# Multiply and GELU over 16 MB: x resident in SBUF, y in a ring, one transfer queue, stores behind all loads

## Chip, core and metric

One core of one Trainium2 chip. The metric is the device time of one execution in microseconds. A ratio is the mean time of one kernel's fast runs over the mean time of the other's fast runs of the same rounds, so it is not quite the ratio of the medians that are quoted.

## The reference

```python
def setup_inputs():
    batch, dim = 1024, 4096
    ...                                   # x and y: float32 [1024, 4096], 16.8 MB each

def reference(x, y):
    z = x * y
    return (0.5 * z * (1 + np.tanh(np.sqrt(2 / np.pi) * (z + 0.044715 * z ** 3)))).astype(np.float32)
```

It is elementwise. 33.55 MB have to come in and 16.78 MB have to go out.

## The kernel before

Each of the 128 partitions holds eight rows of the input, 32768 numbers (128 KiB). The kernel walks over them in seven tiles of 4096 columns and four of 1024. Loads are issued by the sync engine, stores by the scalar engine, and the framework places the semaphores.

```python
def _process_tile(nc, sbuf, tile_f, x_r, y_r, out_r, c0, c1):
    ts_ = c1 - c0
    x_tile = sbuf.tile([128, tile_f], x_r.dtype)
    y_tile = sbuf.tile([128, tile_f], y_r.dtype)
    nc.sync.dma_start(out=x_tile[:, :ts_], in_=x_r[:, c0:c1])
    nc.sync.dma_start(out=y_tile[:, :ts_], in_=y_r[:, c0:c1])
    nc.vector.tensor_mul(out=x_tile[:, :ts_], in0=x_tile[:, :ts_], in1=y_tile[:, :ts_])
    nc.scalar.activation(out=x_tile[:, :ts_], in_=x_tile[:, :ts_],
                         func=mybir.ActivationFunctionType.Gelu_apprx_tanh)
    nc.scalar.dma_start(out=out_r[:, c0:c1], in_=x_tile[:, :ts_])

    # ... in the kernel:
    big_sbuf = ctx.enter_context(tc.tile_pool(name="big", bufs=3))      # 4096 columns: 16 KB rows
    small_sbuf = ctx.enter_context(tc.tile_pool(name="small", bufs=8))  # 1024 columns: 4 KB rows
    # seven big tiles, then four small ones
```

## Time and profile before

| | before |
|---|---|
| time, median of 3 | 123.86 us (123.77 to 123.91) |
| span of the profiled execution | 122.5 us |
| DMA queues | 2 (loads, stores) |
| data packets | 2688 of 16 KB, 1536 of 4 KB |
| vector / scalar engine busy | 29% / 25% |

The span is divided into 40 slices; a digit is the busy share in tenths. GB/s counts a packet's bytes in the slice in which the packet starts. The lines themselves stand in the prediction.

### The profile page before, as it was taken

How to read it: one execution, taken by the hardware profiler on the slowest of the kernel's cores; microseconds unless marked ns; L12 is line 12 of the kernel's file. 1: busy time of each engine (PE TensorE's matmuls, PEld its weight loads, DVE VectorE, ACT ScalarE, POOL GpSimd, SP SyncE). 2: the span in 40 equal slices, each digit the busy share in tenths (PEclk: the TensorE clock that was granted, in tenths of full speed). 3: DMA queues.
4: the chain of work that ended last, by engine and by line, in shares of the span. 5: the costliest groups of instructions: out<-in, count | busy, mean ns of one | idle time of the engine just before them, and what ended most of it. 6: DMA issues, size and time to landing. Idle time of an engine off the chain costs nothing.

```text
span 122.5 us, 134 instructions
## 1 busy us (share of the span) xinstructions
DVE 35.8 (29%) x11; ACT 30.7 (25%) x12; POOL 0.2 (0%) x4
## 2 busy tenths in 40 slices
DVE  0000770590000580068000085019300039555000
ACT  4000029009100019001900004700650000884200
POOL 0000000000000000000000000000000000000000
DMA  4999999989999999999999999999999999999994
GB/s 112 428 433 428 439 439 433 369 337 439 439 433 428 433 428 428 428 433 428 428 433 439 439 433 433 428 428 433 433 428 428 428 417 407 411 413 455 397 423 164
DMA packets 4752, 50.33 MB, mean 411 GB/s; under 512 B 528, under 2 KB 528, under 8 KB 2064
## 3 DMA queue, kind: packets, MB, share of 16 engines
q1 hardware_dynamic: 3168, 33.56, 65.7%
q10 hardware_dynamic: 1584, 16.78, 32.2%
HBM read 33.55 MB, written 16.78 MB: 411 GB/s over the span
## 4 chain that ended last, share of the span: by engine, by line
DMA 76%; DVE 8%; ACT 7%; SPq 1%; issue 1%; DVEq 0%
DMA y_tile<-in_y_dram 30%; DMA out_dram<-x_tile 24%; DMA x_tile<-in_x_dram 22%; DVE x_tile L18 8%; ACT x_tile L20 7%; SPq L15 1%; SPq L16 0%; DVEq L18 0%
## 5 line engine op out<-in xcount | busy, mean ns | idle before, releaser
L18 DVE TENSOR_TENSOR x_tile<-x_tile,y_tile 128x4096 f32<-128x4096 f32 (+1 forms) x11 | 35.8, 3261 | 77.4 <-DMA y_tile<-in_y_dram 77.4
L20 ACT ACTIVATE x_tile<-x_tile 128x4096 f32<-128x4096 f32 (+1 forms) x11 | 29.4, 2684 | 82.8 <-DVE x_tile L18 82.4
L20 ACT ACT_TABLE_LOAD x1 | 1.3, 1283 | 0.7 <-PEq L87 0.7
L87 POOL MEMSET const-bfloat16-1.0<- 128x1 bf16 x1 | 0.1, 101 | 0.0
L87 POOL MEMSET const-uint8-127<- 128x1 uint8 x1 | 0.1, 101 | 0.0
L87 POOL MEMSET const-float32-0.0<- 128x1 f32 x1 | 0.1, 98 | 0.2 <-issue 0.2
L87 POOL MEMSET const-float32-1.0<- 128x1 f32 x1 | 0.1, 98 | 0.0
## 6 DMA issues: line engine op xcount, KB each, us to landing
x_tile<-in_x_dram SPq DMA_DIRECT2D x7, 2048.0 KB, 16.3
y_tile<-in_y_dram SPq DMA_DIRECT2D x7, 2048.0 KB, 20.7
out_dram<-x_tile ACTq DMA_DIRECT2D x7, 2048.0 KB, 13.8
x_tile<-in_x_dram SPq DMA_DIRECT2D x4, 512.0 KB, 21.2
y_tile<-in_y_dram SPq DMA_DIRECT2D x4, 512.0 KB, 20.5
out_dram<-x_tile ACTq DMA_DIRECT2D x4, 512.0 KB, 8.6
```

The costliest lines, as they stand in the source:

```text
L15: nc.sync.dma_start(out=x_tile[:, :ts_], in_=x_r[:, c0:c1])
L18: nc.vector.tensor_mul(out=x_tile[:, :ts_], in0=x_tile[:, :ts_], in1=y_tile[:, :ts_])
L20: nc.scalar.activation(out=x_tile[:, :ts_], in_=x_tile[:, :ts_], func=mybir.ActivationFunctionType.Gelu_apprx_tanh,)
L87: nc = _bacc.Bacc("TRN2", target_bir_lowering=False, num_devices=1)
```

## The change

The intent: rows as long as possible, fewer packets, no second queue, no store between loads. All of x stays in SBUF and is overwritten in place by the result. Only y needs a ring (of 16384 columns), whose two halves are loaded again after the multiplies that read them. Waits are written by hand inside one critical section.

```diff
-    nc.sync.dma_start(out=x_tile[:, :ts_], in_=x_r[:, c0:c1])
-    nc.sync.dma_start(out=y_tile[:, :ts_], in_=y_r[:, c0:c1])
-    nc.vector.tensor_mul(...)
-    nc.scalar.activation(...)
-    nc.scalar.dma_start(out=out_r[:, c0:c1], in_=x_tile[:, :ts_])
+X_LOADS = [(0, 16384), (16384, 32768)]
+Y_LOADS = [(0, 16384, 0), (16384, 24576, 0), (24576, 32768, 8192)]   # columns, place in the ring
+STEP = 4096
+STORES = [(0, 16384), (16384, 32768)]
 ...
+    with tc.tile_critical(no_gpsimd_drain=True):
+        xs = nc.alloc_sbuf_tensor("xs", [P, total_f], F32).ap()
+        ys = nc.alloc_sbuf_tensor("ys", [P, Y_RING], F32).ap()
 ...
+        load_x(0)
+        load_y(0)
+        load_x(1)
+        for i in (1, 2):
+            nc.sync.wait_ge(sem_mul, (Y_LOADS[i][1] - Y_LOADS[1][0]) // STEP)
+            load_y(i)
 ...
+            for c in range(a, b, STEP):
+                nc.vector.tensor_mul(...).then_inc(sem_mul, 1)
+                nc.scalar.wait_ge(sem_mul, n)
+                nc.scalar.activation(...).then_inc(sem_act, 1)
+        for i, (a, b) in enumerate(STORES):
+            nc.sync.wait_ge(sem_act, b // STEP)
+            nc.sync.dma_start(out=out_r[:, a:b], in_=xs[:, a:b]).then_inc(sem_o[i], 16)
```

More of the change, by code (lines that the diff above doesn't have):

```diff
@@ L7 @@
 from concourse._compat import with_exitstack
-def _process_tile(nc, sbuf, tile_f, x_r, y_r, out_r, c0, c1):
-    ts_ = c1 - c0
-    x_tile = sbuf.tile([128, tile_f], x_r.dtype)
-    y_tile = sbuf.tile([128, tile_f], y_r.dtype)
-    nc.sync.dma_start(out=x_tile[:, :ts_], in_=x_r[:, c0:c1])
-    nc.sync.dma_start(out=y_tile[:, :ts_], in_=y_r[:, c0:c1])
-    nc.vector.tensor_mul(out=x_tile[:, :ts_], in0=x_tile[:, :ts_], in1=y_tile[:, :ts_])
-    nc.scalar.activation(
-        out=x_tile[:, :ts_],
-        in_=x_tile[:, :ts_],
-        func=mybir.ActivationFunctionType.Gelu_apprx_tanh,
-    )
-    nc.scalar.dma_start(out=out_r[:, c0:c1], in_=x_tile[:, :ts_])
+F32 = mybir.dt.float32
+GELU = mybir.ActivationFunctionType.Gelu_apprx_tanh
+X_LOADS = [(0, 16384), (16384, 32768)]
+Y_LOADS = [(0, 16384, 0), (16384, 24576, 0), (24576, 32768, 8192)]
+STEP = 4096
+STORES = [(0, 16384), (16384, 32768)]
+Y_RING = 16384
 @with_exitstack
@@ L44 @@
     total_f = x_r.shape[1]
-    big_tiles = [4096] * 7
-    small_tiles = [1024] * 4
-    if sum(big_tiles) + sum(small_tiles) != total_f:
-        big_tiles = []
-        remaining = total_f
-        while remaining >= 4096 * 2:
-            big_tiles.append(4096)
-            remaining -= 4096
-        small_tiles = []
-        while remaining > 0:
-            ts_ = min(1024, remaining)
-            small_tiles.append(ts_)
-            remaining -= ts_
-    big_f = max(big_tiles) if big_tiles else 1024
@@ L61, with load_x, load_y @@
-    small_f = max(small_tiles) if small_tiles else 1024
-    big_sbuf = ctx.enter_context(tc.tile_pool(name="big", bufs=3))
-    small_sbuf = ctx.enter_context(tc.tile_pool(name="small", bufs=8))
-    c0 = 0
-    for ts_ in big_tiles:
-        _process_tile(nc, big_sbuf, big_f, x_r, y_r, out_r, c0, c0 + ts_)
-        c0 += ts_
-    for ts_ in small_tiles:
-        _process_tile(nc, small_sbuf, small_f, x_r, y_r, out_r, c0, c0 + ts_)
-        c0 += ts_
+    with tc.tile_critical(no_gpsimd_drain=True):
+        xs = nc.alloc_sbuf_tensor("xs", [P, total_f], F32).ap()
+        ys = nc.alloc_sbuf_tensor("ys", [P, Y_RING], F32).ap()
+        sem_x = [nc.alloc_semaphore(f"sem_x{i}") for i in range(len(X_LOADS))]
+        sem_y = [nc.alloc_semaphore(f"sem_y{i}") for i in range(len(Y_LOADS))]
+        sem_o = [nc.alloc_semaphore(f"sem_o{i}") for i in range(len(STORES))]
+        sem_mul = nc.alloc_semaphore("sem_mul")
+        sem_act = nc.alloc_semaphore("sem_act")
+        def load_x(i):
+            a, b = X_LOADS[i]
+            nc.sync.dma_start(out=xs[:, a:b], in_=x_r[:, a:b]).then_inc(sem_x[i], 16)
+        def load_y(i):
+            a, b, r = Y_LOADS[i]
+            nc.sync.dma_start(
+                out=ys[:, r : r + b - a], in_=y_r[:, a:b]
+            ).then_inc(sem_y[i], 16)
+        load_x(0)
[4 more added lines that the diff above has]
+            load_y(i)
+        n = 0
+        for i, (a, b, r) in enumerate(Y_LOADS):
+            for j, (xa, xb) in enumerate(X_LOADS):
+                if xa <= a < xb:
+                    nc.vector.wait_ge(sem_x[j], 16)
+            nc.vector.wait_ge(sem_y[i], 16)
+            for c in range(a, b, STEP):
+                nc.vector.tensor_mul(
+                    out=xs[:, c : c + STEP],
+                    in0=xs[:, c : c + STEP],
+                    in1=ys[:, r + c - a : r + c - a + STEP],
+                ).then_inc(sem_mul, 1)
+                n += 1
+                nc.scalar.wait_ge(sem_mul, n)
+                nc.scalar.activation(
+                    out=xs[:, c : c + STEP], in_=xs[:, c : c + STEP], func=GELU
+                ).then_inc(sem_act, 1)
+        for i, (a, b) in enumerate(STORES):
+            nc.sync.wait_ge(sem_act, b // STEP)
+            nc.sync.dma_start(out=out_r[:, a:b], in_=xs[:, a:b]).then_inc(sem_o[i], 16)
+        for i in range(len(STORES)):
+            nc.sync.wait_ge(sem_o[i], 16)
```

## The prediction

> **What bounds the kernel now.** I read the page first, for who is busy, then the rates in chosen stretches, then the chain and the waits to see who waits for whom. The slices and the traffic, from the page:
>
> ```profile
> DVE  0000770590000580068000085019300039555000
> ACT  4000029009100019001900004700650000884200
> ...
> DMA  4999999989999999999999999999999999999994
> GB/s 112 428 433 428 439 439 433 369 337 439 439 433 428 433 428 428 428 433 428 428 433 439 439 433 433 428 428 433 433 428 428 428 417 407 411 413 455 397 423 164
> DMA packets 4752, 50.33 MB, mean 411 GB/s; under 512 B 528, under 2 KB 528, under 8 KB 2064
> ...
> HBM read 33.55 MB, written 16.78 MB: 411 GB/s over the span
> ```
>
> The two compute engines work in islands (29% and 25% of the span); the 16 DMA engines are full from the second slice to the last but one. The bytes are exactly x, y and the output once each, so none can be saved. What is left to gain is the distance between the mean of 411 GB/s and the plateau of about 430. The dips are in the first slice, in slices 8 and 9, from slice 33 on, and in the last. Rates in stretches (columns: stretch, its length, busy time of vector, scalar and pool engine with instructions, clock, DMA share, GB/s):
>
> ```profile
> 0.00:5.00 5.00, 0.00 (x0) 1.28 (x1) 0.20 (x4) 1.00 0.70 239
> 5.00:21.00 16.00, 4.42 (x1) 3.45 (x1) 0.00 (x0) 1.00 1.01 432
> 21.00:28.00 7.00, 4.42 (x1) 0.83 (x2) 0.00 (x0) 1.00 0.99 370
> 28.00:97.00 69.00, 17.70 (x4) 17.42 (x5) 0.00 (x0) 1.00 1.01 431
> 98.00:111.00 13.00, 8.01 (x4) 5.92 (x4) 0.00 (x0) 1.00 1.02 419
> 111.00:115.00 4.00, 1.22 (x1) 1.81 (x2) 0.00 (x0) 1.00 1.00 428
> 116.50:120.25 3.75, 0.00 (x0) 0.00 (x0) 0.00 (x0) 1.00 1.02 419
> ```
>
> 5 to 21 holds loads alone, 28 to 97 loads and stores mixed, 111 to 115 stores of 16 KB rows alone: 432, 431, 428. Loads, stores and a mixture share one limit; they don't add up to more, and mixing costs nothing visible. In 98 to 111 (loads of 4 KB rows) and from 116 (stores of 4 KB rows) it is 419. The dip at 21 to 28 is where the first store is issued:
>
> ```profile
> 21.20 0.38 ACTq L26 DMA_DIRECT2D out_dram<-x_tile  x1
> ```
>
> The chain of waits is made of transfers, and what the vector engine waits for is a landing y:
>
> ```profile
> DMA 76%; DVE 8%; ACT 7%; SPq 1%; issue 1%; DVEq 0%
> ...
> L18 DVE TENSOR_TENSOR x_tile<-x_tile,y_tile 128x4096 f32<-128x4096 f32 (+1 forms) x11 | 35.8, 3261 | 77.4 <-DMA y_tile<-in_y_dram 77.4
> ```
>
> The 8% and 7% of compute in that chain are no cost: while they run, other transfers keep the DMA full. The load queue's own waits, 78.7 us for stores that must free a buffer, look alarming, but the DMA share of 1.01 in the same stretches says that enough was always queued. So the bound is DMA throughput, and the time is bytes over line rate plus a few losses.
>
> **What the Trainium skill says.** "DMA: Bandwidth & Descriptors", section "Where 436 GB/s comes from", derives 16 ports x 32 B x 850 MHz = 435.2 GB/s; this trace's 431 to 432 fits just beneath it. The same section lets HBM bind HBM-to-SBUF traffic at about 358; the trace's 432 contradicts that for this lone core, and the measurement decides. The same page, section "Issuing engines are not separate DMA queues", says that transfers issued from different engines interleave on the same 16 DMA engines; the trace agrees (432 with one queue active, 431 with two). So going to one queue neither gains nor loses rate. "SBUF — State Buffer", section "SBUF size: 192, 224, or 256?", leaves about 208 KiB usable per partition: all of x (128 KiB) and the 64 KiB ring are 192 KiB and fit, which is why y alone needs a ring; no trace shows this. "ScalarE: Activation LUTs", section "What ACT_TABLE_LOAD costs", gives 186 ns + 0.833 ns per element with immediates, 3.60 us for 4096; the trace's 3.616 us agrees, and these instructions don't change.
>
> **The change, part by part.** First the ledger of the present span against the line rate of 435.2. Bytes: 50.33 MB / 435.2 = 115.65 us. Start: 0 to 5 us shows 239 GB/s = 1.195 MB, but a packet counts where it starts, so about half of 16 packets of 16 KB (0.13 MB) belongs later; 1.06 MB are 2.45 us of work, so 2.55 us are lost (0.73 until the first issue, the rest is the way to the first packet and its long first service). Plateau: 16 us at 432 lose 0.12, 69 us at 431 lose 0.67. The dip: 7 us x (1 - 370/435.2) = 1.05. Small tiles: 13 us at 419 lose 0.48; the rest of the end to 120 about 0.3. Sum 5.2, so at 120.8 the DMA engines are done on average; from there to the end of 122.5 are 1.7 us. In the trace the last packet ends at 121.27, its landing is reported at 121.75, and barriers fill the last 0.79.
>
> Larger rows. A 16 KB packet takes 16 x 16384 / 432 = 606.8 ns on its engine, of which 602.4 are the line rate: 4.5 ns fixed (estimate). A 4 KB packet at 419 takes 156.4, of which 150.6 are the line rate: 5.8 ns. So about 5 ns per packet, whatever its size. Before there are 2688 + 1536 data packets, 264 per engine: 1.3 us. After, if a row stays one packet: five transfers of 128 rows of 64 KB and two of 32 KB, 896 rows, 56 per engine: 0.3 us. Gain 1.0 us. It lies on the bounding path throughout, because the engines are always busy.
>
> The first store moved behind all loads, into the same queue. The dip of 1.05 us (about 1.0 beyond the plateau's own loss) follows the first DMA that the scalar engine's queue ever issued. The later stores that begin after a pause show no dip: those issued at 49.23 and 61.28 fall into slices 18 and 22 with 433 and 439. I choose to read it as a first use of that queue, which the change does away with: gain 1.0 us. It is the least certain term, since it could be the first write to HBM instead.
>
> One queue, in order. Is it ever empty? Data flows from about 2.6 us at 434 GB/s: y0 is in by 2.6 + 16.8/0.434 = 41 us, x1 by 60.5, y1 by 70, y2 by 80, the first store by 99. y1 needs two multiplies after y0 (41 + 2 x 4.43 = 50, slack 10 us), y2 four (59, slack 11), the first store the fourth GELU (59 + 3.6 = 63, slack 17), the last store the eighth: 80 + 2 x 4.43 + 3.62 = 93, about 1 us more for landing notices, slack 5 us before 99. No bubble. Eleven multiplies and GELUs become eight equal ones, all hidden.
>
> Start and end. First issue, first packet and its latency stay: 2.55. The end: a smaller spread of the 16 engines with one queue (-0.15), perhaps one more barrier at the end of the hand-placed section (+0.2): 1.75 instead of 1.7.
>
> Sum after: 2.55 + 115.65 + 0.3 (packets) + 0.05 (completion writes) + 1.75 = 120.3 us of span. The unprofiled time before is 123.86 - 122.54 = 1.32 above the span; kept, this gives **121.6 us**, 1.8% faster.
>
> **The rivals.**
> 1. The dip comes back where loads turn to stores, near 80 us. For it: the dip of before coincides with the first write of any kind, and slices 8 and 9 show slow loads before a store's data moves. Against: later returns to storing cost nothing. Time 122.6.
> 2. Rows of 64 KB are cut into packets of 16 KB or less. Against: rows of 16 KB are one packet today (2688 packets for 21 transfers of 128 rows). Cut to 16 KB: 192 per engine x 5 ns = 0.96, so +0.65, 122.3; cut to 32 KB: +0.2.
> 3. Compute is exposed, because loads and stores no longer overlap and the first multiply waits until 41 us instead of 13.09. Against: every slack above is over 4 us, and mixing bought no bandwidth. Were the last store late after all, each us of lateness would be a us of time, 124 or more.
> 4. The two queues' mixture itself was a loss, or the hand-placed semaphores shorten the path noticeably. Against: 431 mixed, 432 alone, and the waits between instructions are hundredths of a us. At most 0.3 us, 121.3.
>
> **Range and chances.** Two per cent below 123.86 is 121.4. The floor of this argument (no barrier added, no spread of the engines, no dip) is 2.5 + 115.65 + 0.35 + 1.27 + 1.32 = 121.1. I give the first-use reading 65%, centred on 121.6 with 0.3 either way; rivals 1 and 2 25%, 122.2 to 122.7; a bubble 5%; something better than my floor 5%. That leaves some 28% under 121.4. Predicted 121.6 us, range 121.0 to 122.6; faster by over 2% 0.28, within 2% 0.70, slower 0.02.
>
> **What would show it.** 896 data packets and 7 x 16 completion writes, about 1010 in all, would confirm the rows; four times as many, rival 2. A rate of about 434 in stretches inside the loads and inside the stores confirms the 5 ns per packet; 431 refutes it. 80 us or so is the place of rival 1: a stretch of 7 us at 370 there is the dip. DMA share at 1.0 from 5 to 118 us confirms that there is no bubble; a chain in which the last store waits for a GELU refutes it. The first rate window, 0 to 5 us, should again lack 2.5 us of work, and the last 1.7 us should look as before. If the start is later because a 64 KB row takes longer to get going, or the gap between span and time is not 1.3 us, the sum is wrong by that much.

## The result

123.41 us (123.32 to 123.48, 4 runs) against 123.83 (123.77 to 123.91, 4 runs): ratio 0.9965, interval 0.9951 to 0.9979. That is the same at 2%, and faster by a third of one per cent. The direction and the class were as predicted; the size was not. 121.6 was forecast with a range of 121.0 to 122.6, so the miss is 1.8 us. All outputs are right.

The page of the kernel after, the lines that answer to those shown of before:

```profile
span 121.6 us, 80 instructions
...
DMA  9777977797789779978999999997997799779970
GB/s 345 345 345 345 690 345 345 345 690 345 345 388 647 345 345 453 582 345 345 431 431 431 431 453 410 345 517 345 431 604 345 345 474 560 345 345 560 474 345 0
DMA packets 1008, 50.33 MB, mean 414 GB/s; under 512 B 112, under 2 KB 112, under 8 KB 112
...
DMA 52%; DVE 22%; ACT 3%; issue 0%; SPq 0%; DVEq 0%
```

1008 packets are 896 rows and 7 x 16 completion writes: a row of 64 KB is one packet, as assumed. The 345s and 690s, and the 7s of the DMA line, are no stutter. A packet of 64 KB takes 2.4 us, a slice 3.04 us, and packets are counted where they start, so a slice sees one or two packets per engine. With such rows the stretch has to be long, or the landings (the moments at which a transfer is reported complete) have to be read instead. The vector engine's instructions give them away, because each group begins when a y lands. From the timeline of the kernel after (start, length, instruction, count, idle time before it and what ended it):

```profile
42.10 17.43 DVE L70 TENSOR_TENSOR xs<-xs,ys 128x4096 f32<-128x4096 f32 x4 [42.10 <-DMA ys<-in_y_dram]
71.16 8.76 DVE L70 TENSOR_TENSOR xs<-xs,ys 128x4096 f32<-128x4096 f32 x2 [11.63 <-DMA ys<-in_y_dram]
81.86 8.76 DVE L70 TENSOR_TENSOR xs<-xs,ys 128x4096 f32<-128x4096 f32 x2 [1.94 <-DMA ys<-in_y_dram]
```

The second part of y (4.19 MB, in the same queue behind x) landed at 71.16, the third (4.19 MB) at 81.86: 10.70 us, where 4.19 MB at 434 GB/s take 9.66. So a full microsecond was lost between the two, shortly before the first store moves. The stretches of the same trace show where (columns as in the prediction):

```profile
40.00:76.00 36.00, 22.27 (x6) 14.85 (x5) 0.00 (x0) 1.00 0.98 422
76.00:83.00 7.00, 5.06 (x2) 6.28 (x2) 0.00 (x0) 1.00 0.99 375
83.00:119.00 36.00, 7.62 (x2) 7.80 (x3) 0.00 (x0) 1.00 1.01 437
```

7 us at 375, with the engines' share at 0.99: they are not idle, their packets are slow. The packet records in the kept trace, which no view prints one by one, show which: 16 load packets of 32 KB, as many as there are engines, start between 77.57 and 77.95 us and take 2.06 us in the mean in place of 1.21. The load packets after them are back at 1.21 to 1.28, and the first store packet, at 80.76, takes the usual 2.42. So the time is lost on loads, about 3 us before a store's data moves. In the kernel before it is much the same: the slow packets, starting from 23.09 to 26.48 us, are all of the load queue, and the first store packet starts at 24.99. This is the dip of before (7 us at 370), moved from 21 to 77 us. It is rival 1 of the prediction. And the first issue is later than the 0.73 us of before:

```profile
0.94 0.38 SPq L48 DMA_DIRECT2D xs<-in_x_dram  x1
```

A third discrepancy is in the times. The prediction added 1.32 us to the span, from a time of 123.86 and a profile of 122.54. But the time of each later run is recorded together with its own span, and time less span is 1.72 to 1.83 in all of them, whatever the kernel; the spans of the kernel before are 121.8 to 122.3 there. So the profile that was studied must have been of an execution about 0.5 us longer than the ones that the 123.86 came from. That half microsecond was counted as something the change would remove.

### The profile page after: what moved, and what is told of

Its sections match the earlier page's. It is cut to its first block, busy times and chain, and to the rows that moved or that the text cites. A ratio compares the mean times of both kernels' runs of the same rounds, so it can differ in the third digit from the quotient of the medians.

```text
span 121.6 us, 80 instructions
## 1 busy us (share of the span) xinstructions
DVE 35.0 (29%) x8; ACT 30.2 (25%) x9; POOL 0.2 (0%) x4
## 2 busy tenths in 40 slices
DMA packets 1008, 50.33 MB, mean 414 GB/s; under 512 B 112, under 2 KB 112, under 8 KB 112
## 3 DMA queue, kind: packets, MB, share of 16 engines
q1 hardware_dynamic: 1008, 50.33, 96.9%
## 4 chain that ended last, share of the span: by engine, by line
DMA 52%; DVE 22%; ACT 3%; issue 0%; SPq 0%; DVEq 0%
DMA ys<-in_y_dram 52%; DVE xs L70 22%; ACT xs L77 3%; SPq L48 0%; DVEq L68 0%; SPq L111 0%; SPq L37 0%
## 5 line engine op out<-in xcount | busy, mean ns | idle before, releaser
L70 DVE TENSOR_TENSOR xs<-xs,ys 128x4096 f32<-128x4096 f32 x8 | 35.0, 4422 | 55.7 <-DMA ys<-in_y_dram 55.7
L77 ACT ACTIVATE xs<-xs 128x4096 f32<-128x4096 f32 x8 | 28.9, 3617 | 63.2 <-DVE xs L70 63.2
```

The lines of the kernel that those rows point to most:

```text
L70: nc.vector.tensor_mul(out=xs[:, c : c + STEP], in0=xs[:, c : c + STEP], in1=ys[:, r + c - a : r + c - a + STEP],).then_inc(sem_mul, 1)
L77: nc.scalar.activation(out=xs[:, c : c + STEP], in_=xs[:, c : c + STEP], func=GELU).then_inc(sem_act, 1)
```

## The experiments

Three theories of the dip were on the table: A, the first write to HBM; B, the turn from loads to stores in one queue; C, the first use of the scalar engine's queue (the prediction's choice). The "turn" is the change from loads to stores. To read the runs, each of them by one profiled execution: in the changed kernel and its variants, the idle time of the vector engine before its last group of multiplies is about 1.9 us with a full dip before the last y landed and about 0.9 without one.

### e1: an early small store in the changed kernel

```diff
+        nc.vector.memset(warm[:, :], 0.0).then_inc(sem_w, 1)            # warm: [128, 128]
+        nc.scalar.wait_ge(sem_w, 1)
+        nc.scalar.dma_start(out=out_r[:, 0:128], in_=warm[:, :]).then_inc(sem_wd, 16)
         load_x(0)
 ...
+        nc.sync.wait_ge(sem_wd, 16)      # before the real stores
```

> The changed kernel with one 64 KB store of zeros into the first output columns, issued on the scalar engine's queue at the very start and waited for before the real stores. Theory A (the dip near 78 us comes from the first write of the kernel to HBM, whatever queue): the dip near 78 us vanishes, its 0.9 us is paid under the start or not at all, time about 122.5 to 122.7 (0.8 us less than 123.4). Theory B (the dip comes from the turn from loads to stores in one queue, or from the first store on the sync queue): the dip stays at 77 to 80 us and the time stays at 123.4 to 123.6.

Measured: 123.55 us (ratio to before 0.9982). The last group of multiplies, in its timeline:

```profile
81.96 8.76 DVE L77 TENSOR_TENSOR xs<-xs,ys 128x4096 f32<-128x4096 f32 x2 [1.86 <-DMA ys<-in_y_dram]
```

The dip stayed. A small first write doesn't pay it off.

### e2, e3, e6: fresh queue or first write, in the kernel before

The making of the tile `warm` is left out of the cuts.

```diff
 e2
+    nc.scalar.dma_start(out=warm[:, :], in_=x_r[:, 0:128])                        # a 64 KB load
 e3, behind the first x and y load
+        nc.sync.dma_start(out=out_r[:, total_f - 128 : total_f], in_=warm[:, :])  # a 64 KB store
 e6, at the start
+    nc.scalar.dma_start(out=out_r[:, total_f - 128 : total_f], in_=warm[:, :])
```

> The kernel before with one 64 KB load issued on the scalar engine's queue at the start, so that this queue is no longer fresh when the first store comes at 21 us. Theory A (first write): the dip at 23 to 26 us stays, time 123.9 to 124.1. Theory C (first use of that queue, the prediction's reading): the dip vanishes, time about 122.9 to 123.1.

> The kernel before with one 64 KB store of zeros on the sync queue behind the first x and y load, so that it runs at about 12 us among loads; the scalar queue stays fresh until 21 us. Theory A (first write): the dip moves to about 9 to 13 us and none is left at 23 to 26; time within 0.2 of 124.0. Theory C (first use of the scalar queue): no dip near 12, the dip stays at 23 to 26.

> The kernel before with one 64 KB store of zeros on the scalar queue at the start. Theory F: the dip at 23 to 26 us vanishes, time 123.1 to 123.4. Theory G: it stays, time 123.9 to 124.1.

Measured: 124.00, 123.97 and 123.93 us, with before at 123.83, 123.83 and 123.79. The stretch of the dip in e2:

```profile
21.00:28.00 7.00, 4.43 (x1) 0.85 (x2) 0.00 (x0) 1.00 1.01 386
```

in e3:

```profile
21.00:28.00 7.00, 4.43 (x1) 0.69 (x2) 0.00 (x0) 1.00 1.01 391
```

and in e6:

```profile
21.00:28.00 7.00, 4.42 (x1) 0.82 (x2) 0.00 (x0) 1.00 1.02 393
```

All three have the dip where it was, 0.6 to 0.7 us deep (7 x (1 - 390/431)), a little less than the 1.0 of the first profile. The queue had carried a load (e2) or a store (e6) already, so C falls. HBM had been written already (e3, e6), so A in its simple form falls as well.

### e5, e7: the same queue, and half a megabyte

Both are the changed kernel without the hand-placed section (e4, below). In e5 a 64 KB store went over the one queue that carries everything. It was meant to be the first transfer, but the framework put it behind the first x load, at about 21 us. In e7 512 KB went over the scalar queue from the start; packets of 4 KB took turns with load packets of 64 KB, so they were spread over 7 to 23 us (packet records).

```diff
 e5
+    nc.sync.dma_start(out=out_r[:, 0:128], in_=warm[:, :])
 e7
+    nc.scalar.dma_start(out=out_r[:, 0:1024], in_=warm[:, :])
```

> The changed kernel without the hand-placed section (122.85 us, run e4), with one 64 KB store of zeros as the first transfer of the sync queue, the queue that carries everything. Theory F (the first store of each queue costs about 0.9 us, and the early stores so far went over the other queue): the dip near 78 us vanishes, time 122.0 to 122.4. Theory G (the first large store costs it, however small ones went before): the dip stays, time 122.9 to 123.2.

> Run e4 with a 512 KB store of zeros (4 KB rows) on the scalar queue at the start; it adds 1.2 us of traffic. Theory G with a threshold that half a megabyte passes: a dip in the first 10 us, none near 78, time about 124.0 or, if the dip hides under the start, 123.3. Theory F or a higher threshold: the dip stays near 78, time about 124.1.

Measured: 122.88 and 123.96 us. The last group in e5:

```profile
81.66 8.76 DVE L53 TENSOR_TENSOR xs<-xs,ys 128x4096 f32<-128x4096 f32 x2 [1.59 <-DMA ys<-in_y_dram]
```

and in e7:

```profile
82.66 8.76 DVE L53 TENSOR_TENSOR xs<-xs,ys 128x4096 f32<-128x4096 f32 x2 [1.58 <-DMA ys<-in_y_dram]
```

The dip stays in both, at 0.7 us. Theory F (each queue's first store) falls. e7 leaves open whether its stores were too few, too slow or in the wrong queue.

### e10, e11: is it once, or at every turn?

```diff
 e10, behind the second x load (at 60 us), then y, then the rest
+    nc.sync.dma_start(out=out_r[:, 0:8192], in_=xs[:, 0:8192])
 e11, behind the first x load (at 21 us)
+    nc.sync.dma_start(out=out_r[:, 0:3072], in_=warm[:, :])        # 1.5 MB of zeros
```

> Run e4 with the first 4 MB of the output stored between the second x load and the third y load (at 60 us), then 19 us of loads, then the rest. Theory N (once per execution): a dip at 57 to 61 us, none at the second turn near 89. Theory P (each start of storing after a long stretch of loads alone): dips at both, time 0.9 us over 122.9, 123.8.

> Run e4 with 1.5 MB of zeros (12 KB rows) stored behind the first x load, at 21 us, in the same queue; 3.6 us more traffic. Theory N: a dip at about 18 to 22 us and none at the turn 55 us later, near 82; time 126.5. Theory P: dips at both, time 127.3.

Measured: 123.11 and 126.89 us. For comparison the same groups in e4, which has no early burst:

```profile
41.89 17.43 DVE L53 TENSOR_TENSOR xs<-xs,ys 128x4096 f32<-128x4096 f32 x4 [41.89 <-DMA ys<-in_y_dram]
...
71.03 8.76 DVE L53 TENSOR_TENSOR xs<-xs,ys 128x4096 f32<-128x4096 f32 x2 [11.71 <-DMA ys<-in_y_dram]
...
81.76 8.76 DVE L53 TENSOR_TENSOR xs<-xs,ys 128x4096 f32<-128x4096 f32 x2 [1.97 <-DMA ys<-in_y_dram]
```

e10:

```profile
81.76 8.76 DVE L53 TENSOR_TENSOR xs<-xs,ys 128x4096 f32<-128x4096 f32 x2 [22.30 <-DMA ys<-in_y_dram]
...
91.45 8.76 DVE L53 TENSOR_TENSOR xs<-xs,ys 128x4096 f32<-128x4096 f32 x2 [0.93 <-DMA ys<-in_y_dram]
```

e11:

```profile
46.85 17.43 DVE L53 TENSOR_TENSOR xs<-xs,ys 128x4096 f32<-128x4096 f32 x4 [42.80 <-DMA ys<-in_y_dram]
...
75.92 8.76 DVE L53 TENSOR_TENSOR xs<-xs,ys 128x4096 f32<-128x4096 f32 x2 [11.63 <-DMA ys<-in_y_dram]
...
85.55 8.76 DVE L53 TENSOR_TENSOR xs<-xs,ys 128x4096 f32<-128x4096 f32 x2 [0.88 <-DMA ys<-in_y_dram]
```

In e10 the second y landed at 81.76. Without the early store it was 71.03 (e4), and 4.19 MB more take 9.66: 80.69. So the early store met the dip (1.07 us late), and the turn 19 us of loads later did not: from 81.76 to 91.45 are 9.69 us. In e11 the first y landed 4.96 us after the 41.89 of e4, for 3.62 us more traffic; the real turn 55 us later shows no dip (85.55 - 75.92 = 9.63). In these runs the cost is paid once per execution, and an earlier burst buys it off. Theory B, in the form of "at every turn", falls.

### e9: small tiles first

```diff
-    for ts_ in big_tiles: ...
-    for ts_ in small_tiles: ...
+    for ts_ in small_tiles: ...
+    for ts_ in big_tiles: ...
```

> The kernel before with its four 1024-column tiles first, so that the first stores are 512 KB and come at about 8 us, mixed with loads. Theory N (the dip belongs to the first start of storing at speed, of any size from half a megabyte): one dip at about 6 to 12 us, none later. Theory S (it comes where a long backlog of loads meets the first large store): dip at the first 2 MB store, near 20 to 30 us. Time between 123.3 and 124.3.

Measured: 130.69 us, far out of what was expected, for a reason that has nothing to do with the dip:

```profile
9.00:15.00 6.00, 2.53 (x3) 2.11 (x2) 0.00 (x0) 1.00 1.06 417
...
35.00:41.00 6.00, 2.92 (x1) 0.00 (x0) 0.00 (x0) 1.00 0.99 401
...
115.00:124.00 9.00, 3.73 (x1) 3.62 (x1) 0.00 (x0) 1.00 0.13 56
```

With a large tile last, its multiply and its GELU (4.4 + 3.6 us) run with nothing left to transfer: 9 us at 56 GB/s. The small tiles at the end of the kernel before earn about 7 us. As for the dip, a weaker one came at the first 512 KB stores and a second at the first 2 MB store, 401 GB/s. So one clean dip was wrong here; with a gentle beginning it comes in two parts.

### e14, e15: rate or volume, write or read

```diff
 e14, in place of the 1.5 MB of e11: 512 KB to HBM
+    nc.sync.dma_start(out=out_r[:, 0:1024], in_=warm[:, :])
 e15: the 1.5 MB of e11, but to SBUF (the second x load overwrites it later)
+    nc.sync.dma_start(out=xs[:, 16384 : 16384 + 3072], in_=warm[:, :])
```

> Run e11 with 512 KB of zeros in place of 1.5 MB (4 KB rows), at full rate at 21 us. If rate sets the dip off, the dip is at 19 to 22 us and none near 79. If volume does (above half a megabyte), none at 21 and one near 79. Time 124.1 to 124.3 either way.

> Run e11 with the 1.5 MB copied from SBUF to SBUF in place of stored to HBM. If bulk reading of SBUF by the DMA engines sets the dip off, it is at 19 to 22 us and none at the turn near 82. If writing to HBM does, none at 21 and one at 82. Time about 126.5 to 127.

Measured: 124.05 and 126.80 us. e14:

```profile
44.39 17.43 DVE L53 TENSOR_TENSOR xs<-xs,ys 128x4096 f32<-128x4096 f32 x4 [42.47 <-DMA ys<-in_y_dram]
...
83.11 8.76 DVE L53 TENSOR_TENSOR xs<-xs,ys 128x4096 f32<-128x4096 f32 x2 [0.89 <-DMA ys<-in_y_dram]
```

e15:

```profile
46.96 17.43 DVE L53 TENSOR_TENSOR xs<-xs,ys 128x4096 f32<-128x4096 f32 x4 [42.91 <-DMA ys<-in_y_dram]
...
85.67 8.76 DVE L53 TENSOR_TENSOR xs<-xs,ys 128x4096 f32<-128x4096 f32 x2 [0.85 <-DMA ys<-in_y_dram]
```

e14: the first y is 2.50 us later than in e4 for 1.21 us of traffic, and the real turn is clean. So half a megabyte is enough if it comes as a burst in the loads' queue; e7 had the same bytes, but spread out, taking turns with loads, and in the scalar queue. No run parts these two differences. The queue alone doesn't decide, since the stores of the kernel before and of e13 (below) go over the scalar queue and meet the dip. e15 is the surprise: before a copy that never writes to HBM, the first y is 5.07 us later for 3.62 of traffic (a packet of the copy takes 0.46 us, as one of e11's stores does), and the turn at 82 us is without a dip. So writing to HBM isn't needed. What e11, e14 and e15 share is a burst of transfers whose source is SBUF, behind a stream of loads. A change of tensor alone isn't enough: in e4 the loads pass from x to y near 22 us at an unchanged 434 GB/s (packet records).

### e17, e18: can it be paid in the slow first microseconds?

```diff
 in the changed kernel, as the very first transfer; e17: 512 columns (256 KB), e18: 1024 (512 KB)
+        nc.sync.wait_ge(sem_w, 1)
+        nc.sync.dma_start(out=xs[:, 16384 : 16384 + W], in_=warm[:, :]).then_inc(sem_wd, 16)
         load_x(0)
         load_y(0)
+        nc.sync.wait_ge(sem_wd, 16)
         load_x(1)
```

> The changed kernel (123.41 us) with a 256 KB copy from SBUF to SBUF as the very first transfer. It costs 0.6 us of traffic and about 0.5 us of later start. If it pays off the dip and the pay-off hides in the slow start of the first loads: no dip near 79, time 123.0 to 123.4. If it pays but does not hide: 124.0 to 124.6. If 256 KB do not set it off: dip near 79, 124.3 to 124.6.

> The same with 512 KB: 1.2 us of traffic and about 1 us of later start. Hidden: 124.0 to 124.5 and no dip near 79; not hidden: 125.0 to 125.5.

Measured: 124.99 and 126.03 us, worse than every expectation. The last group of e18:

```profile
84.50 8.76 DVE L77 TENSOR_TENSOR xs<-xs,ys 128x4096 f32<-128x4096 f32 x2 [2.17 <-DMA ys<-in_y_dram]
```

The dip is there in full, and e17's last group, with 1.69 us of idle time before it, has most of it. 512 KB in a burst ahead of the first load bought nothing off, while 512 KB behind a load did (e14). So the burst has to come behind a running stream of loads, as far as these two runs show; e14 stored to HBM and e18 copied to SBUF.

### e4: the changed kernel without the hand-placed section

```diff
-    with tc.tile_critical(no_gpsimd_drain=True):
-        xs = nc.alloc_sbuf_tensor("xs", [P, total_f], F32).ap()
-        ... (all semaphores, wait_ge and then_inc)
+    xs = xp.tile([P, total_f], F32)      # xp, yp: pools with one buffer
+    ys = yp.tile([P, Y_RING], F32)
     # the same transfers, multiplies and GELUs in the same order
```

> The changed kernel's same transfers and instructions, with the semaphores placed by the framework in place of the hand-placed section. The span should lose 0.2 us at its start (first issue 0.94 to 0.73) and about 0.3 us at its end, 121.1; the dip stays. Theory D (the section also causes the 0.47 us by which time less span grew, 1.32 to 1.79): time about 122.4. Theory E (that growth belongs to the transfers, for instance to the last large store or to the one queue): time about 122.9, the difference stays near 1.8.

Measured: 122.85 us (122.80 to 123.00, 5 runs), ratio to before 0.9926 (0.9914 to 0.9938). The span is 121.2, and the first issue is back where it was:

```profile
0.73 0.38 SPq L44 DMA_DIRECT2D xs<-in_x_dram  x1
```

The section cost 0.56 us: 0.2 at the start, where each engine first waits for a signal of the sync engine, and the rest at the end, where a further round of drains follows the last store (from the last packet's end to the end of the span are 1.55 us with the section and 1.15 without). Of the two theories of the 0.47 us, E came closer in number (122.9), but neither was right: there was no growth to explain, since time less span is 1.8 in every kernel.

### e8, e16, e12: what the long rows are worth

e8 is e4 with every transfer in 16 KB rows; e16 repeats it. e12 has 16 KB rows only around the turn.

```diff
 e8, e16
-X_LOADS = [(0, 16384), (16384, 32768)]
+X_LOADS = [(c, c + 4096) for c in range(0, 32768, 4096)]      # Y_LOADS and STORES likewise
 e12
+Y_LOADS = [(0, 16384, 0), (16384, 24576, 0), (24576, 28672, 8192), (28672, 32768, 12288)]
+STORES = [(c, c + 4096) for c in range(0, 16384, 4096)] + [(16384, 32768)]
```

> Run e4 with all transfers cut to 16 KB rows (eight loads of x, eight of y, eight stores; same order in the same queue). If a packet costs 4.5 to 5 ns besides its bytes, 192 packets per engine in place of 56 cost 0.6 to 0.7 us: time 123.5, rates of 431 in place of 434. If the rows do not matter, 122.9. The dip stays in either case.

> Run e8 again. If the small dip of e8 (0.25 us) was chance, the dip is now 0.6 to 1.0 and the time 123.4 to 123.6. If it belongs to this layout, the dip is again near 0.3 and the time 123.1.

> Run e4 with 16 KB rows only around the turn: the last 4 MB of y as two loads, the first 8 MB of stores as four. If what made the dip small in run e8 (0.25 us in place of 1.0) is the row size at the turn, the dip is 0.3 and the time 122.3 to 122.5, the best so far. If it was something else in run e8, the dip stays near 1.0 and the time is 122.9 to 123.1.

Measured: 123.09 us (e8), 122.93 (e16), 123.06 (e12); e4 had 122.85. Stretches of e4:

```profile
5.00:40.00 35.00, 0.00 (x0) 1.28 (x1) 0.00 (x0) 1.00 1.00 433
...
76.00:83.00 7.00, 5.03 (x2) 6.28 (x2) 0.00 (x0) 1.00 1.01 375
```

and of e8:

```profile
5.00:40.00 35.00, 11.40 (x3) 6.61 (x2) 0.00 (x0) 1.00 1.00 429
...
76.00:83.00 7.00, 5.82 (x3) 5.56 (x2) 0.00 (x0) 1.00 0.99 410
```

With 64 KB packets such a stretch is uncertain by what starts at its ends (e4 reads 433 from 5 to 40 us, but 422 from 40 to 76 and 437 from 83 to 119). If the packet records are used to spread each packet's bytes over its own duration, e4 has 433.4 GB/s outside the dip (6 to 76 and 84 to 118 us) and e8 430.0, so the rows do raise the rate about as forecast; over 107 us that is 0.8 us. But the dip of e8 is 0.33 us (7 x (1 - 410/430)) where e4 has 0.94, and e16 confirms it (407 GB/s). So some 0.6 us of the rows' gain are given back in a deeper dip. The times show the remaining 0.1 to 0.2, which isn't clear of noise: the ratios to the kernel before are 0.9926, 0.9942 and 0.9936, with overlapping intervals. e12 shows that the row size just around the turn isn't what does it: with 16 KB rows there, the stretch stayed at 377 GB/s. Why e8 and e16 have the small dip stays open.

### e13: stores mixed with loads

```diff
             nc.scalar.activation(out=xs[:, c : c + STEP], ...)
+            nc.scalar.dma_start(out=out_r[:, c : c + STEP], in_=xs[:, c : c + STEP])
-    for a, b in STORES: nc.sync.dma_start(...)
```

> Run e4 with eight 2 MB stores on the scalar queue, each as soon as its GELU is done, so mixed with the loads from 50 us on. If the order of stores and loads is worth nothing, the time is that of e4 plus 32 more packets per engine... eight stores of 16 KB rows have 64 packets per engine in place of 16, 0.2 us: 123.0 to 123.2, with a dip near 47 to 52 us. If stores behind all loads are worth something by themselves, over 123.5. If a gentler start avoids the dip, 122.2 to 122.4.

Measured: 123.09 us, 0.24 more than e4, as expected for the added packets. So nothing is left that putting the stores behind all loads would be worth by itself. Nor did mixing avoid the dip: by the packet records its loss sat in two pieces, at 53 to 56 and 60 to 63 us, 0.9 us together.

## Why the prediction was wrong

The step that failed most is "**The first store moved behind all loads ... gain 1.0 us**". The dip was read as the first use of the scalar queue and given 65%. It stayed, at 1.0 us, because it belongs to something that the change keeps: the first time a burst of transfers out of SBUF follows on a stream of loads. Rival 1 named the right place and the right size, though not the right cause: it spoke of a first write, and e15 shows the dip before any write to HBM. The inner mechanism isn't settled. The runs say what sets it off (a burst, with SBUF as its source, behind loads; 512 KB is enough, 64 KB and e7's slow 512 KB aren't), that it comes once, if in two pieces in e9 and e13, and that it falls on the loads just ahead of the burst. They don't say why.

The second is "**The unprofiled time before is 123.86 - 122.54 = 1.32 above the span; kept**". The difference of time and span is a constant, but it is 1.72 to 1.83. The two numbers came from different executions. Taken as 1.78, this alone moves the forecast by 0.46 us. Seen the other way, the ledger started from a span 0.5 us longer than usual, and part of what it promised to save wasn't there in most runs.

The third is "**Start and end. First issue, first packet and its latency stay**", with 0.2 us for a barrier. The section cost 0.56 in all (e4): the issue moved from 0.73 to 0.94, which had been taken as fixed, and the end was undersized.

Together: 121.6 + 1.0 (dip) + 0.46 (offset) + 0.56 - 0.2 (section) = 123.4, the measured 123.41. That it fits to a hundredth is luck, since the dip alone reads 0.85 us by the packets and 1.04 by the landings. The class "within 2%" was no test either: it reaches from 121.4 to 126.3 us and would have held with the dip or without.

Two readings of the prediction were loose, without harm to its sum. The stretch 98 to 111 us isn't loads of 4 KB rows alone: 76 store packets of 16 KB start in it, but 116.5 to 120.25, which has 4 KB packets only, gives the same 419. And the stores issued at 49.23 and 61.28 us fall into slices 17 and 21 (428 and 433 GB/s), not 18 and 22; there is no dip there either.

What held: the rows stay one packet each (1008 packets), the rate rose from 431 to 433 and more, and there is no bubble: the last GELU ends at 94.3, almost 6 us before the first store is through, near 100. As a rate the gain of the rows had about the predicted size; as time most of it went into the deeper dip, where rows of 64 KB were compared with rows of 16 KB in the same order (e8, e16). What the removed small tiles gained was not measured by itself. The rivals of exposed compute and of cut rows fell as said, and mixing stores with loads costs nothing beyond its packets (e13). So the expected gain went to three places: 0.6 us are paid to the section, one microsecond that was to be saved was only moved, and half a microsecond was never there.

The lowest median is that of e4: the same transfers with the framework's semaphores, 122.85 us, 0.7% under before (ratio 0.9926), and under the changed kernel's 123.41. e16, with rows of 16 KB, is within noise of it (122.93).

## What to carry to other kernels

When the DMA engines are full from end to end, moving a loss to another time doesn't remove it: before you book a dip as gained, ask what sets it off and whether the new order still does that. Take a time and a span from the same execution before you subtract one from the other, and look at several executions before a ledger goes below a half per cent. Longer rows are worth at most one or two tenths of a per cent here, and a hand-placed section can cost more than they bring. Where each tile is stored when it is done, end with small tiles whose compute is short (e9: 7 us).

## What the Trainium skill lacked or had wrong

- "DMA: Bandwidth & Descriptors" (and every other page read for this) lacks the one-off loss: once per execution, when a burst of transfers from SBUF first follows on a stream of loads, load packets just ahead of it are slowed and 0.3 to 1.5 us are lost (e8, e10, e11, e14, e15). 512 KB of copy from SBUF ahead of any load doesn't pay for it (e18).
- "DMA: Bandwidth & Descriptors", section "Where 436 GB/s comes from", says that for HBM-to-SBUF transfers the HBM side binds at about 358 GB/s. The one core that this program uses sustained 431 with 16 KB rows and 433 with 64 KB rows, within 1% of that section's 435.2; no run here loads both cores of a pair. The page "HBM Reference", section "Specifications (TRN2)", has the better figure for a core alone, about 425.
- "DMA: Bandwidth & Descriptors", section "Measured (HBM→SBUF, 128 partitions, SWDGE, issued from GpSimd)", puts a packet's minimum at about 10.5 ns, for a 4 KB transfer issued from GpSimd. That is not what a row of 4 or 16 KB costs beyond its bytes when the sync or scalar engine issues it, for which no page has a figure in ns: 4.5 to 6 ns here, an estimate from 432 GB/s at 16 KB and 419 at 4 KB against 435.2.
- No page says what a hand-placed section costs at its start and end: 0.56 us here (123.41 against 122.85).
